# Background work of a two-block transformer kernel is spread over more steps

## The chip, the cores and the metric

The kernel runs on one core of one Trainium2 chip. The metric is the device time of one execution in microseconds (us); lower is better. Times before are the median of three executions, and one further execution was recorded by the hardware profiler.

## The reference, cut to what matters

256 tokens of 1024 features pass through two blocks. The first block has two layers; each is feed-forward, mixer, feed-forward. A feed-forward is `h + 0.5 * (silu(u @ w1) * (u @ w3)) @ w2` with 2816 inner features, on a normalised `u`. So there are four feed-forwards in the first block, here called feed-forward 0 to 3.

The second block has two layers over the tokens and over 256 context tokens. Each starts with a modulation:

```python
mod   = split_cols((sc @ w_mod[l] + b_mod[l])[:, None, :], (D_MODEL,) * N_MOD)
mod_x = split_cols(sc_ctx @ w_mod[l] + b_mod[l], (D_MODEL,) * N_MOD)
```

`sc` and `sc_ctx` are two vectors of 1024 numbers, `w_mod[l]` is 1024 x 6144. The result (table l: shifts, scales and gates) does not depend on the tokens, so it can be computed long before it is used. The same holds for the second block's other tables: the position biases, the sinks and the constants of its layer norms. All arithmetic is fp32.

## The kernel before, in words

**Weights.** All large matrices lie in one stream of 540 tiles of 128x1024, which `Weights` loads by SP's DMA queue into three buffers (`wst`, L270). `prepare` splits each tile into a high part `whi` (ScalarE, ACT, L279) and a low part `wlo` (VectorE, DVE, L280), both kept four deep. `mm3` multiplies a block of 128x128 with three matmuls, high by high, high by low and low by high (L324 to L326).

**A feed-forward of the first block** (`ffn1_layer`) has 22 up steps j, each two weight tiles (48 matmuls), one scaling (L863), a product (L866) and a split of the result (ACT L330, DVE L331), and 8 down steps m with 66 matmuls each and an eviction (L797). After each j and each m it calls `step()`, 30 calls in all; `drain()` at the end calls it until nothing is left.

**Background work.** `step()` advances every generator in `bg` by one `yield`. What a generator issues in a step is placed behind marks: on each engine behind the last split of the layer, on the matmul engine behind the last matmul. Beyond that the compiler's scheduler orders each engine's queue; it may put later independent work first.

- `late_gen` (feed-forward 0) waits four steps, then loads constants and tables. Its three `oneh` tiles share the four buffers `mw` of the modulation. `replicate(0)` then issues eight DMAs of 384 KB on ACT's queue.
- `later_gen` (feed-forward 1) loads the sinks, issues eight such DMAs (`replicate(1)`, read in the odd mixer) and four of 349 KB (`rrep`, read in the second block), and then computes layer-norm constants in small pieces (DVE, and matmuls L458 and L480).
- `mod_gen` computes a table. For table 0 it runs in feed-forwards 0, 1 and 2, with 2048 columns in each, in two groups of 1024 columns (CW). For every 128 rows of a group (k = 0 to 7) it loads a tile `mw` (SP, L708), multiplies by `sc` and adds into the accumulator `macc` on DVE (L724), and does the same for `sc_ctx` with a product on ACT (L727) and an addition on GpSimd (POOL, L728). At k = 0 both products go to ACT (L722). One `yield` follows each k, one follows the group, and then the sum over partitions is taken by matmuls with ones (L736), evicted (L739) and written to DRAM (`modrow`, L741), with one more `yield`: ten steps a group. After the last group the rows are read back (`mt`), transposed (L753) and finished as `modv` and `s1p` (L756 to L761).

**Table 1** is computed in the second block's `ffn2_layer(0)` by `mod_gen(gp, 1, 0, 6 * D, 512, 3)`: twelve groups of 512 columns; the pool gives `macc` one buffer. There a whole group (all eight k) is one step, so that a group has three. That layer calls `step()` 38 times: 6 + 5 + 8 + 11 times in up and down projections and 8 times in `down_gen([0])`. Then come:

```python
            self.drain()
            pre = [self.double_prep(l, 1, 1, 0, i) for i in both]
            self.weave((self.double_gen(l, 1, stats[0], pre[0]), self.DL_STEPS),
                       (self.down_gen([1], gh, gl, evict(True)), KB))
```

`double_prep` reads `modv` and `s1p` of table 1 and makes small weights `dl_w` by transposes (L1320, L1321). `double_gen` turns the statistic of the tokens' rows into `dl_c` (L1340), `rows` and at last the split inputs `HI` and `LO` (L1412, L1413) that the next layer's first weights multiply. `down_gen([1])` is the context's down projection, 264 matmuls that need none of this. Evictions of both down projections are L1543 (`ex` for the tokens, `cx` for the context).

Of the kernel before, what the change touches and what calls it, by code (L numbers as in the profile page):

```python
# [292 lines left out]
class Body:  # L293
# [143 lines left out]
    def later_gen(self):  # L437

        nc, a = self.nc, self.a
        c = self.const  # L440
        self.sink = c.tile([128, 16], FT, name="sink")
        nc.scalar.dma_start(self.sink, _ap(a["row"], ROW_SINK, [[0, 128], [1, 16]]))
        yield
        yield from self.replicate(1)
        self.rrep = self.dram.tile([64, 2 * 6 * 15 * 31], FT, name="rrep")
        for q in range(4):
            nc.scalar.dma_start(self.rrep[16 * q:16 * q + 16], _ap(a["rpb"], 0, [[0, 16], [1, 5580]]))
            yield
        self.nsink = c.tile([128, 16], FT, name="nsink")
        nc.vector.tensor_scalar(self.nsink, self.sink, -1.0, None, op0=OP.mult)  # L450

        ps = self.ps("st")
        o = _VEC["ln1_b"]
        nc.tensor.matmul(ps[:, :32], self.ones, self.vec[:, o:o + 32], start=True, stop=True)
        self.nbb = c.tile([128, 4], FT, name="nbb")
        nc.vector.tensor_reduce(self.nbb, ps[:, :32].rearrange("p (a b) -> p a b", b=8), AX.X, OP.add)
        nc.vector.tensor_scalar(self.nbb, self.nbb, -1.0 / D, None, op0=OP.mult)
        yield  # L458

        self.lnc = c.tile([128, 3, KB, 8], FT, name="lnc")  # L460
        nc.vector.memset(self.lnc, 0.0)
        self.lk = c.tile([128, 3, 4], FT, name="lk")
        for s, (l, which) in enumerate(self.PAIRS):
            g, b = self.ln_cols(l, which)
            w = self.w1()[:, :KB * 4].rearrange("p (m q) -> p m q", q=4)
            nc.vector.tensor_scalar(w[:, :, 0], g, 1.0 / D, None, op0=OP.mult)
            nc.vector.tensor_tensor(w[:, :, 1], w[:, :, 0], g, op=OP.mult)
            nc.vector.tensor_scalar(w[:, :, 3], b, self.nb(l, which), None, op0=OP.add)
            nc.vector.tensor_tensor(w[:, :, 2], w[:, :, 0], w[:, :, 3], op=OP.mult)
            nc.vector.scalar_tensor_tensor(w[:, :, 3], w[:, :, 3], 1.0 / D, w[:, :, 3], op0=OP.mult, op1=OP.mult)  # L470
            lc = self.lnc[:, s]
            for j in (0, 4):
                nc.vector.tensor_scalar(lc[:, :, j], self.ones[:, :KB], 1.0 / D, None, op0=OP.mult)
            nc.vector.tensor_copy(lc[:, :, 1], w[:, :, 0])
            nc.vector.tensor_scalar(lc[:, :, 2], w[:, :, 1], -2.0, None, op0=OP.mult)
            nc.vector.tensor_scalar(lc[:, :, 3], w[:, :, 2], 2.0, None, op0=OP.mult)
            nc.vector.tensor_copy(lc[:, :, 5], w[:, :, 1])
            yield
            ps = self.ps("st")
            nc.tensor.matmul(ps[:, :32], self.ones, w.rearrange("p m q -> p (m q)"), start=True, stop=True)  # L480
            nc.vector.tensor_reduce(self.lk[:, s], ps[:, :32].rearrange("p (m q) -> p q m", q=4), AX.X, OP.add)
            for q, f in ((0, -1.0), (2, -2.0)):
                nc.vector.tensor_scalar(self.lk[:, s, q:q + 1], self.lk[:, s, q:q + 1], f, None, op0=OP.mult)
            yield
        self.rsel = c.tile([32, 3, 128], FR, name="rsel")
        for j, q in enumerate((0, 5, 6)):
            nc.vector.tensor_tensor(self.rsel[:, j], self.ident[:32, q:q + 1].to_broadcast([32, 128]),
                                    self.ident[:32, q + 7:q + 8].to_broadcast([32, 128]), op=OP.add)

        self.lsel = c.tile([128, 8], FT, name="lsel")  # L490
        for k in range(2):
            nc.vector.tensor_tensor(self.lsel[:, 4 * k:4 * k + 4], self.ident[:, 32 * k:32 * k + 4],
                                    self.ident[:, 32 * k + 64:32 * k + 68], op=OP.add)
        self.cc = c.tile([128, 2, 3, 32], FT, name="cc")
        nc.vector.memset(self.cc, 0.0)
        yield
# [196 lines left out]
    def mod_gen(self, pool, l, c0, c1, CW, nb, wait=0):  # L693

        nc = self.nc
        for _ in range(wait):
            yield
        gs = list(range(c0, c1, CW))
        if l:
            gs = gs[4:8] + gs[:4] + gs[8:]  # L700
        todo = [(g, k) for g in gs for k in range(KB)]
        ws = []

        def load():
            if todo:
                g, k = todo.pop(0)
                ws.append(pool.tile([128, CW], FT, name="mw", bufs=nb))
                nc.sync.dma_start(ws[-1], self.a["wmod"][l, k * 128:(k + 1) * 128, g:g + CW])  # L708

        for _ in range(nb - 1):  # L710
            load()
        yield
        for g in gs:
            n = 2 if l == 0 or g < 2 * D else 1
            acc = pool.tile([128, 2, CW], FT, name="macc")
            for k in range(KB):
                load()
                w = ws.pop(0)
                for i in range(n):
                    s = self.sc[:, i * 8 + k:i * 8 + k + 1]  # L720
                    if k == 0:
                        nc.scalar.activation(acc[:, i], w, AF.Copy, scale=s)  # L722
                    elif i == 0:
                        nc.vector.scalar_tensor_tensor(acc[:, i], w, s, acc[:, i], op0=OP.mult, op1=OP.add)  # L724
                    else:
                        t = pool.tile([128, CW], FT, name="mp", bufs=2)
                        nc.scalar.activation(t, w, AF.Copy, scale=s)  # L727
                        nc.gpsimd.tensor_tensor(acc[:, i], acc[:, i], t, op=OP.add)  # L728
                if CW == 1024 or k == KB - 1:
                    yield  # L730
            yield
            w = CW * n // 4
            rows = [(i, c) for i in range(n) for c in range(0, CW, w)]
            ps = self.ps("st")
            for p, (i, c) in enumerate(rows):
                nc.tensor.matmul(ps[32 * p:32 * p + 32, :w], self.ones[:, :32], acc[:, i, c:c + w], start=True,  # L736
                                 stop=True, tile_position=(0, 32 * p), skip_group_check=True)
            mr = self.w2(1)[:, 0, :w]
            nc.scalar.activation(mr, ps[:, :w], AF.Copy)  # L739
            for p, (i, c) in enumerate(rows):  # L740
                nc.sync.dma_start(self.rowd[l][i:i + 1, g + c:g + c + w], mr[32 * p:32 * p + 1])  # L741
            yield
        if c1 == 6 * D:
            mt = pool.tile([128, CW], FT, name="mt", tag="mp", bufs=2)[:96, :128]
            if n == 2:
                nc.sync.dma_start(mt, self.rowd[l].rearrange("i (k c) -> (i k) c", c=128))
            else:
                nc.vector.memset(mt, 0.0)
                nc.sync.dma_start(mt[:48], self.rowd[l][0:1].rearrange("i (k c) -> (i k) c", c=128))
                nc.sync.dma_start(mt[48:64], self.rowd[l][1:2, :2048].rearrange("i (k c) -> (i k) c", c=128))  # L750
            yield
            ps = self.ps("st")
            nc.tensor.transpose(ps[:, :96], mt, self.ident[:96, :96])  # L753
            b = self.vec[:, _VEC["b_mod"] + 48 * l:_VEC["b_mod"] + 48 * l + 48]
            mv = self.modv[l].rearrange("p (i c) -> p i c", i=2)
            nc.vector.tensor_tensor(mv, ps[:, :96].rearrange("p (i c) -> p i c", i=2),  # L756
                                    b[:, None, :].to_broadcast([128, 2, 48]), op=OP.add)
            for half in range(2):
                c = 24 * half + 16
                nc.vector.tensor_scalar(mv[:, :, c:c + 8], mv[:, :, c:c + 8], 1.0 / ALPHA, None, op0=OP.mult)  # L760
                nc.vector.tensor_scalar(self.s1p[l][:, :, half], mv[:, :, 24 * half + 8:24 * half + 16], 1.0, None,  # L761
                                        op0=OP.add)
            yield
# [74 lines left out]
    def ffn1_layer(self, st, nxt, slot, name, idx):  # L838
        nc = self.nc
        with self.tc.tile_pool(name="g" + name, bufs=1) as gp, self.tc.tile_pool(name="mod" + name, bufs=1) as mp:  # L840
# [4 lines left out]
            if idx == 3:  # L845
                self.bg.append(self.ctx_init())
            if idx < 3:
                self.bg.append(self.mod_gen(mp, 0, 2 * D * idx, 2 * D * (idx + 1), 1024, 4, 6 if idx == 0 else 0))
            gh = gp.tile([128, FB, S], FR, name="ghi")
            gl = gp.tile([128, FB, S], FR, name="glo")  # L850
            for j in range(FB):
# [1174 lines left out]
```

## Time and profile before

| | |
|---|---|
| median of 3 executions | 2060.02 us (2059.41 to 2060.64) |
| profiled execution | 2062.72 us, its span 2060.9 us |
| granted clock of the matmul engine, mean | 0.988 |
| HBM read | 351.66 MB, 175 GB/s over the span |

The views used are the page (busy shares of each engine), the windows (busy time, instruction counts, granted clock and DMA share of a stretch), the waits (who released an idle engine), the groups by form (mean duration of one kind of instruction) and the timeline. In a window, "(x694)" after PE is the number of its matmuls.

### The profile page before, as it was taken

The page shows a single profiled execution, that of the slowest core. Times are in us where ns is not written, and L with a number is a line of the kernel's source. Part 1 is how long each engine was busy: PE and PEld are TensorE (multiplying, and loading weights), DVE is VectorE, ACT ScalarE, POOL GpSimd, SP SyncE. Part 2 cuts the span into 40 slices and gives each one's busy share as a digit, 9 for nine tenths or more (in the row PEclk, how much of TensorE's full clock was granted, in tenths as well). Part 3 has the DMA queues.
Part 4 walks back from the last instruction along what each step waited for, and adds up shares of the span by engine and source line. Part 5 has one row for each costly group of instructions (what it writes and reads, how often), then busy time and mean ns, then how long its engine had stood idle before and what let it go on. Part 6 is the DMA issues. An engine that isn't in the chain of part 4 may idle for free. (4 is left out here: it accounts for less than half of the span.)

```text
span 2060.9 us, 39210 instructions
## 1 busy us (share of the span) xinstructions
PE 1989.5 (97%) x15355; PEld 1851.9 (90%) x15355; DVE 1524.9 (74%) x2680; ACT 1134.6 (55%) x2028; POOL 408.4 (20%) x305
## 2 busy tenths in 40 slices
PE   8998999999999999999999999999999999989997
PEld 8988999989999998999999777988888889869997
DVE  6797797998599768886686978666665679776554
ACT  5464587555466548555556866533443455855443
POOL 1223041321033111210330112302230013112002
PEclk9999999999999999999999999999999999999999
DMA  6785645876577563556642323475555653125553
GB/s 219 260 266 171 202 144 184 281 249 215 185 232 229 187 216 110 184 172 188 188 145 73 104 80 118 144 250 169 160 163 164 216 169 103 50 83 156 183 183 103
DMA packets 117114, 355.39 MB, mean 172 GB/s; under 512 B 21782, under 2 KB 27625, under 8 KB 116481
## 3 DMA queue, kind: packets, MB, share of 16 engines
q1 hardware_dynamic: 115472, 344.54, 51.9%
q10 hardware_dynamic: 1456, 8.36, 1.1%
q8 instruction: 120, 1.97, 0.4%
q14 instruction: 66, 0.53, 0.1%
HBM read 351.66 MB, written 8.90 MB: 175 GB/s over the span
## 5 line engine op out<-in xcount | busy, mean ns | idle before, releaser
L280 DVE TENSOR_TENSOR wlo<-wst,whi 128x1024 fp32r<-128x1024 f32 x540 | 709.2, 1314 | 329.4 <-ACT whi L279 327.1
L324 PE MATMUL mm<-HI,whi 128*128 128x256 f32 (+1 forms) x2944 | 865.2, 296 | 12.7 <-ACT whi L279 8.4
L326 PE MATMUL mm<-HI,wlo 128*128 128x256 f32 (+1 forms) x2944 | 863.9, 294 | 6.0 <-DVE wlo L280 6.0
L325 PE MATMUL mm<-LO,whi 128*128 128x256 f32 (+1 forms) x2944 | 865.4, 295 | 1.0 <-DVE LO L1413 0.9
L279 ACT ACTIVATE whi<-wst 128x1024 fp32r<-128x1024 f32 x540 | 570.2, 1056 | 524.8 <-PE mm L325 292.7
L324 PEld LDWEIGHTS mm<-HI,whi 128*128 128x128 f32 x2944 | 564.2, 193 | 38.3 <-issue 11.4
L326 PEld LDWEIGHTS mm<-HI,wlo 128*128 128x128 f32 x2944 | 566.1, 192 | 21.8 <-DVE wlo L280 7.3
L325 PEld LDWEIGHTS mm<-LO,whi 128*128 128x128 f32 x2944 | 566.6, 193 | 18.7 <-issue 6.9
L326 PE MATMUL mm<-ghi,wlo 128*128 128x256 f32 (+1 forms) x1000 | 289.1, 289 | 4.7 <-DVE wlo L280 4.7
L324 PE MATMUL mm<-ghi,whi 128*128 128x256 f32 (+1 forms) x1000 | 287.7, 289 | 1.3 <-ACT ghi L330 1.3
L325 PE MATMUL mm<-glo,whi 128*128 128x256 f32 (+1 forms) x1000 | 288.6, 289 | 0.2 <-DVE glo L331 0.2
L728 POOL TENSOR_TENSOR macc<-macc,mp 128x1024 f32<-128x1024 f32 (+1 forms) x70 | 167.9, 2398 | 447.2 <-ACT mp L727 298.1
L326 PEld LDWEIGHTS mm<-ghi,wlo 128*128 128x128 f32 x1000 | 192.8, 193 | 8.4 <-DVE wlo L280 5.1
L324 PEld LDWEIGHTS mm<-ghi,whi 128*128 128x128 f32 x1000 | 192.4, 193 | 4.3 <-issue 1.5
L325 PEld LDWEIGHTS mm<-glo,whi 128*128 128x128 f32 x1000 | 192.7, 193 | 2.8 <-issue 1.1
L724 DVE SCALAR_TENSOR_TENSOR macc<-mw,sc,macc 128x512 f32<-128x512 f32 (+1 forms) x126 | 168.3, 1336 | 25.6 <-DMA mw<-in_wmod 20.4
L325 PE MATMUL mm<-wlo,HI 128*128 128x256 f32 x352 | 100.6, 286 | 4.0 <-DVE wlo L280 4.0
L324 PE MATMUL mm<-whi,HI 128*128 128x256 f32 x352 | 101.1, 288 | 0.0
L326 PE MATMUL mm<-whi,LO 128*128 128x256 f32 x352 | 100.2, 286 | 0.0
L727 ACT ACTIVATE mp<-mw,sc 128x1024 f32<-128x1024 f32 (+1 forms) x70 | 67.4, 973 | 27.5 <-DMA mw<-in_wmod 18.5
L527 POOL TENSOR_TENSOR sacc<-sacc,w 128x256 f32<-128x256 f32 x36 | 33.6, 932 | 236.7 <-ACT w L523 235.5
L330 ACT ACTIVATE ghi<-w 128x256 fp32r<-128x256 f32 (+1 forms) x120 | 51.1, 426 | 49.8 <-DVE w L866 47.1
(425 smaller groups left out, 2502.5 us busy)
## 6 DMA issues: line engine op xcount, KB each, us to landing
wst<-in_wall SPq DMA_DIRECT2D x540, 512.0 KB
mw<-in_wmod SPq DMA_DIRECT2D x48, 512.0 KB
mw<-in_wmod SPq DMA_DIRECT2D x96, 256.0 KB
brep<-bvec ACTq DMA_DIRECT2D x16, 384.0 KB
nab<-rrep SPq DMA_DIRECT2D x24, 96.0 KB
bias<-brep SPq DMA_DIRECT2D x4, 512.0 KB
bias<-brep SPq DMA_DIRECT2D x8, 256.0 KB
rrep<-in_rpb ACTq DMA_DIRECT2D x4, 348.8 KB
```

The source lines that it names most:

```text
L279: self.marks.append(self.nc.scalar.activation(hi, src, AF.Copy))
L280: self.nc.vector.tensor_tensor(lo, src, hi.bitcast(FT), op=OP.subtract)
L324: nc.tensor.matmul(ps, wh, xh, start=first, stop=False, skip_group_check=True)
L325: nc.tensor.matmul(ps, wh, xl, start=False, stop=False, skip_group_check=True)
L326: self.last = nc.tensor.matmul(ps, wl, xh, start=False, stop=last, skip_group_check=True)
L330: self.marks = [self.nc.scalar.activation(hi, src, AF.Copy), self.nc.vector.tensor_tensor(lo, src, hi.bitcast(FT), op=OP.subtract)]
L527: nc.gpsimd.tensor_tensor(st["acc"], st["acc"], sq, op=OP.add)
L724: nc.vector.scalar_tensor_tensor(acc[:, i], w, s, acc[:, i], op0=OP.mult, op1=OP.add)
L727: nc.scalar.activation(t, w, AF.Copy, scale=s)
L728: nc.gpsimd.tensor_tensor(acc[:, i], acc[:, i], t, op=OP.add)
```

## The change

Two waiting steps instead of six ahead of the modulation in feed-forward 0; a step without work after k = 2 and after k = 5 of a group of 1024 columns; one more step between the end of a group (of any width) and its sum; six steps without work in `later_gen` after its first DMA.

```diff
@@ later_gen
         nc.scalar.dma_start(self.sink, _ap(a["row"], ROW_SINK, [[0, 128], [1, 16]]))
         yield
+        for _ in range(6):
+            yield
         yield from self.replicate(1)
@@ mod_gen
                 if CW == 1024 or k == KB - 1:
                     yield
+                if CW == 1024 and k in (2, 5):
+                    yield
+            yield
             yield
             w = CW * n // 4
@@ ffn1_layer
-                self.bg.append(self.mod_gen(mp, 0, 2 * D * idx, 2 * D * (idx + 1), 1024, 4, 6 if idx == 0 else 0))
+                self.bg.append(self.mod_gen(mp, 0, 2 * D * idx, 2 * D * (idx + 1), 1024, 4, 2 if idx == 0 else 0))
```

## Rows read from the trace of the kernel before

**Rows 1.** The page's first part: busy time, share of the span, instructions.

```profile
PE 1989.5 (97%) x15355; PEld 1851.9 (90%) x15355; DVE 1524.9 (74%) x2680; ACT 1134.6 (55%) x2028; POOL 408.4 (20%) x305
```

**Rows 2.** Windows: us, then PE, PEld, DVE, ACT, POOL busy, PEclk, DMA, GB/s.

```profile
80.00:180.00 100.00, 89.61 (x694) 86.33 (x693) 94.44 (x85) 56.66 (x75) 40.84 (x14) 0.95 0.70 236
400.00:500.00 100.00, 90.79 (x720) 87.03 (x719) 89.94 (x137) 53.30 (x72) 25.40 (x10) 0.97 0.71 239
580.00:680.00 100.00, 99.33 (x820) 97.32 (x819) 95.74 (x96) 60.66 (x81) 41.66 (x14) 1.00 0.72 227
1880.00:1980.00 100.00, 100.00 (x836) 100.00 (x835) 54.56 (x70) 46.48 (x70) 0.00 (x0) 1.00 0.57 184
```

**Rows 3.** Waits of PE in 80 to 180 and 400 to 500: total us, times, longest.

```profile
PE mm L326 <- DVE wlo L280: 9.0, 5, 3.5
...
PE st L480 <- DVE w L470: 5.0, 3, 2.3
```

**Rows 4.** Groups by form on DVE, last layer; L863 from 80 to 180.

```profile
L280 DVE TENSOR_TENSOR wlo<-wst,whi 128x1024 fp32r<-128x1024 f32 x35 | 42.9, 1225 | 46.2 <-ACT whi L279 46.2
L1509 DVE TENSOR_TENSOR w<-w,mm 128x256 f32<-128x256 f32 x18 | 7.5, 414 | 0.0
L331 DVE TENSOR_TENSOR glo<-w,ghi 128x256 fp32r<-128x256 f32 x17 | 7.1, 419 | 0.0
...
L863 DVE TENSOR_TENSOR w<-mm,rstd 128x512 f32<-128x512 f32 x12 | 8.2, 679 | 0.1
```

**Rows 5.** Timeline of DVE in feed-forward 0: start, duration, instruction.

```profile
94.58 1.27 DVE L724 SCALAR_TENSOR_TENSOR macc<-mw,sc,macc 128x1024 f32<-128x1024 f32 x1
...
99.32 3.43 DVE L724 SCALAR_TENSOR_TENSOR macc<-mw,sc,macc 128x1024 f32<-128x1024 f32 x1
```

**Rows 6.** Timeline of POOL in feed-forwards 1 and 2.

```profile
371.03 2.44 POOL L728 TENSOR_TENSOR macc<-macc,mp 128x1024 f32<-128x1024 f32 x1 [18.96 <-ACT mp L727]
...
413.11 2.35 POOL L728 TENSOR_TENSOR macc<-macc,mp 128x1024 f32<-128x1024 f32 x1 [3.60 <-ACT mp L727]
...
592.43 3.31 POOL L728 TENSOR_TENSOR macc<-macc,mp 128x1024 f32<-128x1024 f32 x1 [3.05 <-ACT mp L727]
598.80 3.31 POOL L728 TENSOR_TENSOR macc<-macc,mp 128x1024 f32<-128x1024 f32 x1 [3.05 <-ACT mp L727]
```

**Rows 7.** Window of feed-forward 0 ahead of the modulation's first group.

```profile
40.00:60.00 20.00, 20.00 (x163) 19.23 (x162) 12.53 (x17) 8.47 (x12) 0.00 (x0) 1.00 0.58 180
```

**Rows 8.** Timeline of PE at the end of down_gen([1]).

```profile
1671.85 0.28 PE L326 MATMUL mm<-ghi,wlo 128*128 128x256 f32 x1
...
1676.46 0.79 PE L1394 MATMUL tp<-rows,dl_w 32*128 32x256 f32 x2 [3.78 <-DVE h L1410]
```

**Rows 9.** Timeline of DVE in ffn2_layer(0), up projection and end.

```profile
1565.01 0.75 DVE L724 SCALAR_TENSOR_TENSOR macc<-mw,sc,macc 128x512 f32<-128x512 f32 x1 [1.08 <-DMA mw<-in_wmod]
...
1631.96 0.48 DVE L1543 SCALAR_TENSOR_TENSOR ex<-mm,modv,ex 128x256 f32<-128x256 f32 x1 [0.30 <-PE mm L326]
...
1653.32 0.26 DVE L756 TENSOR_TENSOR modv<-st,vec 128x96 f32<-128x96 f32 x1 [0.50 <-PE st L753]
...
1661.78 0.16 DVE L1340 COPY dl_c<-tp 128x16 f32<-128x16 f32 x1
...
1677.34 0.90 DVE L1413 TENSOR_TENSOR LO<-h,HI 128x256 fp32r<-128x256 f32 x1
```

**Rows 10.** Timeline of PE: the sums of table 1's last three groups.

```profile
1602.31 0.43 PE L736 MATMUL st<-macc,ones 128*32 128x128 f32 x8
...
1624.29 0.42 PE L736 MATMUL st<-macc,ones 128*32 128x128 f32 x8
...
1644.06 0.43 PE L736 MATMUL st<-macc,ones 128*32 128x128 f32 x8
```

**Rows 11.** Timeline of ACT: a group's first product, and the small weights.

```profile
1553.64 0.70 ACT L722 ACTIVATE macc<-mw,sc 128x512 f32<-128x512 f32 x1
...
1660.29 1.08 ACT L1321 ACTIVATE dl_w<-tp 96x512 fp32r<-96x512 f32 x2
```

## The prediction

> **What bounds the kernel now.** The page's busy shares come first: TensorE (PE) is busy 97% of the span, VectorE (DVE) 74% [rows 1]. So time can only come from stretches in which PE is short of work, and the next view is the windows. In the last layer, where nothing runs beside the weights, PE issues 836 matmuls in 100 us, 0.1196 us each, with no idle time [rows 2]; a step of the up projection (48 matmuls) is 5.74 us. In the three layers that carry the first modulation (table 0), the same 100 us hold 694, 720 and 820 matmuls [rows 2], while DVE is busy 94, 90 and 96 us instead of 55. PE stands idle there for 10.4, 9.2 and 0.7 us, and the granted clock falls to 0.95 and 0.97 after these stops: parts of the windows ran at 1.2 GHz instead of 2.4. The waits name the releasers: the split weights wlo in the first layer, the later tables' small DVE work in the second [rows 3]. DVE is thus what limits PE in these stretches, and only there.
>
> Why DVE is late: without modulation a step needs two splits of 1.225 us, 0.68 for the up pair's scaling, 0.41 and 0.42 for product and split [rows 4], 3.96 us of the 5.74. A modulation step adds one DVE multiply-add, 1.27 us alone, but 3.43 when it meets the GpSimd (POOL) add of the step before [rows 5]. What a full step then takes is read from POOL's adds: six intervals from 371.03 to 413.11 us, 7.01 us each, in the second layer; 6.37 us in the third [rows 6].
>
> **The change, part by part.**
>
> *Rests in a group of 1024 columns (all three layers).* Before, steps k=1 to 7 follow each other: at 7.01 us DVE falls behind by 1.27 a step, 8.9 us in seven, and only then come two light steps. At 6.37 us it is 0.63 a step, 4.4 us in seven, and that layer loses only 16 matmul slots (1.9 us) [rows 2, 6]: some 4 to 5 us of backlog is carried by the split tiles that lie ready. After, a light step gives back 5.74 - 3.96 = 1.78: k=1,2 reach 2.5, the rest leaves 0.8, k=3 to 5 reach 4.6, the rest leaves 2.8, k=6,7 reach 5.3, and three light steps (one is the sum's new wait) give back 5.3. The peak is what the third layer carries now, so nearly all stops should go. Their worth: idle 20.3 us plus the clock, 5% and 3% of 100 us, together 28.3 us; by slots 142 + 116 + 16 = 274, times 0.1196, 32.8 us, which includes the sums' own matmuls that stay. I take a gain of **28 us** (ends: 10, from rival D, and 33). What is late next in these layers is PE itself.
>
> *First layer: two waiting steps instead of six.* The group's 16 weight loads and their work begin four steps sooner, beside the constants' loads. DVE is busy 12.5 of 20 us there and the DMA engines 0.58 [rows 7], so both have room. late_gen's three oneh tiles come out of the same four buffers as the modulation's weights, now while these are in use; a load may then wait a step, and two rests take that up. Nothing, -1 to +2 us. The start is needed, since the two groups now take 26 steps; 2 + 1 + 26 = 29 fit in the layer's 30. The modulation's loads share SP's queue with the weights; a load whose buffer DVE or ACT still reads holds the weight load behind it, and with DVE less late these stops get shorter. POOL's queue holds the same adds, spread wider; the next norm's small adds stand behind them only in the down projection.
>
> *Second layer: later_gen six steps later.* Twelve DMAs on the ACT queue (brep, rrep) and the small DVE and PE pieces move from steps 2 to 21 to 8 to 27. The readers come layers later, so nothing waits. The pieces behind PE's 5.0 us of waits [rows 3] then stand half in the down projection, whose steps are 66 matmuls (7.9 us). That is in the 28.
>
> *Second block: the sum's extra wait is not tied to 1024 columns.* This is the price. mod_gen for table 1 has 512 columns, twelve groups of three steps: 1 + 36 + 1 = 38, exactly the 38 steps of ffn2_layer(0), with the last transpose drained. Now a group has four: the ninth sum (group 8) falls on step 37, group 9's multiply-adds on step 38, and drain() issues that sum, both remaining groups and the transpose. Behind it stand double_prep, which reads modv, and double_gen, whose LO the next block's first slabs need; the only other PE work is down_gen([1]). The cover is small: its last matmul starts at 1671.85, and PE then waits 3.78 us for DVE already [rows 8].
>
> Worked out: step 37 ends with the seventh of down_gen([0])'s m-steps, whose eviction is at 1631.96 [rows 9]; group 8's sum comes there. Three rounds follow in series, because one accumulator (macc) must be summed before the next group's first product. Rounds now, sum to sum, take 21.98 and 19.77 us [rows 10]. The multiply-adds alone, in a calmer stretch, run from 1553.64 to 1565.76, 12.1 us [rows 9, 11]; the rest of a round is the sum, which waits its turn in PE's order. I take 17 for the two rounds beside down_gen([1]), between 12.5 and 20.9, and 12 for the last, when PE and the DMA engines are free: 46. Sum to modv is 9.3 us now (1644.06 to 1653.32) [rows 9, 10]: two short DMAs, one after the other, and a transpose that stands among matmuls; with PE free I take 6.7. From modv to the first LO is 24.0 us now (1653.32 to 1677.34), dl_w at 1660.29 and dl_c at 1661.78 on the way [rows 9, 11]. Weight splits, evictions and down_gen([1])'s matmuls stand between in every queue, and LO does not come before the last of those. With them gone I take 15 (ends 12 and 24). LO: 1632 + 46 + 6.7 + 15 = 1699.7, against 1677.3: a loss of **22 us** (ends: 1632 + 37.5 + 6.7 + 12 gives 11; 1632 + 62.7 + 9.3 + 24 gives 51). Nothing of the next block can fill it. The clock after so long a stop: nothing, 0 to 3, since PE stops there now as well.
>
> *Sum.* The profiled execution took 2062.7 us (span 2060.9), 2.7 above the median of the runs, 2060.0. 2062.7 - 28 + 22 = 2056.7; on the median's scale **2054**.
>
> **The rivals.** A measurement of this kernel can tell about 0.2%, 4.1 us, so "same" is 2055.9 to 2064.1.
>
> *B, the drain costs more (slower).* Place: the three rounds at the end of ffn2_layer(0). If they keep today's 20.9 us, R is 62.7, the loss 39, and the time 2060 - 28 + 39 = 2071. It decides from a mean round of 17.2 us on (with my other terms the loss is three rounds less 23.6, and 28 is then reached). For it: both rounds in that stretch are longer [rows 10], and down_gen([1]) loads as many weights as down_gen([0]). Against: the multiply-adds themselves need 12.1 us, and the last round runs alone.
>
> *C, the drain is half hidden (faster still).* If double_gen's statistics, which read nothing of modv, are put ahead of the late modulation and the rounds run at 12.5, then modv to LO is about 10 us and the loss 37.5 + 6.7 + 10 - 45.3 = 9: 2041. For it: the instruction order is the scheduler's, not the program's alone. Against: dl_c follows dl_w now [rows 9, 11], though it needs only a finished statistic, as if PSUM tiles of one tag were handed out in the program's order.
>
> *D, the rests are too few (slower).* If every POOL add costs DVE its own 2.4 us whole [rows 6], a full step is 3.96 + 1.27 + 2.40 = 7.63, the backlog grows by 1.89 a step and reaches 9.7 us in the new pattern; 4.4 above the 5.3 that I take as carried, in four groups, is 18 us. Gain 10, time 2060 - 10 + 22 = 2072. This is what the Trainium skill's page "SBUF — State Buffer" (section "Who interferes with whom") would make of it: a DVE instruction with two SBUF inputs and a GpSimd one that reads SBUF exclude each other for a whole instruction. The trace agrees for single instructions (1.27 against 3.43), but the step of 6.37 us says that much of it falls into time that DVE or POOL wait anyway.
>
> **How the numbers follow.** My case 0.50 (own range, by gains of 25 to 31 and losses of 17 to 29, 2046 to 2064; faster 0.34, same 0.13, slower 0.03); B 0.22 (slower 0.20, same 0.02); C 0.12, faster; D 0.16 (slower 0.12, same 0.04). Faster 0.46, same 0.19, slower 0.35. The range takes in the middles of B, C and D: 2039 to 2075.
>
> **What would show it.** Right: about 820 matmuls or more in the 100 us windows of the first two layers, clock 1.00, waits for wlo and L480 gone; against it a PE gap of some 25 us near the end of ffn2_layer(0), modv about 53 us after the eviction at which group 8's sum stands (now 21), ended by h or LO. Wrong: windows that stay near 720 (D), rounds of over 18 us (B), or modv early enough that PE waits under 10 us (C).

## The result and the profile after

The changed kernel takes 2079.77 us (median of 6 runs, 2074.46 to 2084.58), the kernel before 2059.72 us (6 runs, 2055.18 to 2062.79): a ratio of 1.0094, 95% interval 1.0079 to 1.0108. The change made the kernel 20 us slower; 2054.0 was forecast, and the range ended at 2075. The profiled execution of the changed kernel took 2075.63 us (span 2073.8, mean granted clock 0.983), 4.1 below its median, that of before 3.0 above its own; so the two traces differ by 12.9 us only. Sizes below are from medians unless a trace is named.

In the changed kernel later lines have moved: L724 is L726, L727 L729, L728 L730, L736 L741, L753 L758, L480 L482, L756 L761, L1413 L1418, L1543 L1548.

The page's first part, of the kernel after (of before: [rows 1]):

```profile
PE 1985.6 (96%) x15355; PEld 1850.5 (89%) x15355; DVE 1524.6 (74%) x2680; ACT 1136.4 (55%) x2028; POOL 406.3 (20%) x305
```

Busy time hardly moved, so the 12.9 us are PE standing idle or slowed. The windows of the three modulation layers come next (columns as in [rows 2]), and one of the end of `ffn2_layer(0)`; kernel after:

```profile
80.00:180.00 100.00, 93.54 (x755) 91.17 (x754) 88.81 (x86) 56.39 (x76) 32.53 (x12) 0.98 0.73 240
400.00:500.00 100.00, 94.71 (x765) 93.33 (x764) 88.42 (x126) 54.47 (x74) 24.99 (x10) 0.97 0.72 241
580.00:680.00 100.00, 100.00 (x834) 99.03 (x833) 91.77 (x96) 60.48 (x82) 29.62 (x10) 1.00 0.72 227
...
1655.00:1700.00 45.00, 18.21 (x125) 12.54 (x124) 26.25 (x87) 12.02 (x29) 7.98 (x7) 0.62 0.35 103
```

The same end in the kernel before:

```profile
1655.00:1700.00 45.00, 41.22 (x332) 37.02 (x331) 36.16 (x114) 24.54 (x53) 9.88 (x9) 0.92 0.53 164
```

The matmuls in the three windows rose from 694, 720 and 820 [rows 2] to 755, 765 and 834: the third layer is full, the first two are repaired in part. What is left there, by the waits of PE (20 to 240 us, then 340 to 560; total us, times, longest), kernel after, against 9.0 and 5.0 [rows 3]:

```profile
PE mm L326 <- DVE wlo L280: 6.6, 5, 3.3
...
PE st L482 <- DVE w L472: 4.0, 1, 4.0
```

At the end of `ffn2_layer(0)` PE issues 125 matmuls in 45 us where it issued 332, at a mean granted clock of 0.62: that is where the gain and more was lost.

To place gains and losses to a few tenths, I counted the large matmuls (L324 to L326), which every kernel here issues in the same number and layer by layer in the same order, and took the start of the n-th in each trace, less its start in the trace of before. The profiled times of all kernels, in us:

```
                    n =   1584   3960   5544  10560  11088    end
                        end of: FFN0   FFN1   FFN2  (ahead of, behind the stop)
before, start           224.9  555.9  752.7 1596.9 1682.5
after                    -6.6  -11.3  -12.9  -16.5  +11.7  +12.8
e1 wide only             -6.1   -9.5  -11.0  -11.8  -11.6  -11.8
e2 narrow alone          -1.6   +1.9   +1.9   -0.5  +26.9  +29.0
e3 tables back           -5.4   -8.3   -9.9  -11.7  -11.0  -11.2
e4 no POOL additions    -16.6  -29.5  -32.9  -35.1  -34.7  -34.9
e5 both on DVE          -15.3  -28.9  -32.3  -34.1  -34.4  -34.6
e6 three rests           -2.8   +0.3   +4.8   +5.6   +4.9   +4.7
e7 e5, fewer steps      -15.9  -29.4  -32.9  -31.1  -36.5  -34.1
e8 before, both on DVE  -16.2  -28.0  -29.1  -31.4  -30.9  -31.2
e9 after, both on DVE   -15.7  -28.7  -32.1  -35.9   -3.5   -2.9
e10 no rests             -8.9  -16.1  -17.8  -19.1  -18.9  -19.2
e11 sum's wait alone     -0.9   -0.1   -1.8   -3.0   -3.6   -3.8
e12 e10, both on DVE    -15.8  -28.2  -30.4  -31.4  -31.4  -31.6
```

Read the line of after: 12.9 us gained over the three layers, 16.5 by 1597 us, and 28.2 lost between matmul 10560 and 11088. Some 2 to 3 of the 3.6 us between the third layer and 1597 us belong to the narrow groups' wait itself: e2, which has nothing else, gains 2.4 there, after 3.6, e1 without that wait 0.8.

### The profile page after: what moved, and what is told of

Read it like the earlier page. It is cut to its first block, busy times and chain, and to the rows that moved or that the text cites. A ratio compares the mean times of both kernels' runs of the same rounds, so it can differ in the third digit from the quotient of the medians.

```text
span 2073.8 us, 39200 instructions
## 1 busy us (share of the span) xinstructions
PE 1985.6 (96%) x15355; PEld 1850.5 (89%) x15355; DVE 1524.6 (74%) x2680; ACT 1136.4 (55%) x2028; POOL 406.3 (20%) x305
## 5 line engine op out<-in xcount | busy, mean ns | idle before, releaser
L324 PE MATMUL mm<-HI,whi 128*128 128x256 f32 (+1 forms) x2944 | 862.5, 295 | 13.3 <-ACT whi L279 8.4
L326 PE MATMUL mm<-HI,wlo 128*128 128x256 f32 (+1 forms) x2944 | 861.5, 294 | 3.6 <-DVE wlo L280 3.6
L324 PEld LDWEIGHTS mm<-HI,whi 128*128 128x128 f32 x2944 | 562.0, 192 | 36.5 <-issue 11.9
L326 PEld LDWEIGHTS mm<-HI,wlo 128*128 128x128 f32 x2944 | 564.0, 192 | 19.2 <-DVE wlo L280 4.7
L326 PE MATMUL mm<-ghi,wlo 128*128 128x256 f32 (+1 forms) x1000 | 289.9, 290 | 6.0 <-DVE wlo L280 6.0
L324 PE MATMUL mm<-ghi,whi 128*128 128x256 f32 (+1 forms) x1000 | 288.6, 289 | 0.2 <-ACT ghi L330 0.2
L730 POOL TENSOR_TENSOR macc<-macc,mp 128x1024 f32<-128x1024 f32 (+1 forms) x70 | 165.8, 2369 | 550.7 <-ACT mp L729 357.4
L326 PEld LDWEIGHTS mm<-ghi,wlo 128*128 128x128 f32 x1000 | 193.1, 193 | 10.8 <-DVE wlo L280 6.8
L324 PEld LDWEIGHTS mm<-ghi,whi 128*128 128x128 f32 x1000 | 192.8, 193 | 5.1 <-issue 3.4
L726 DVE SCALAR_TENSOR_TENSOR macc<-mw,sc,macc 128x512 f32<-128x512 f32 (+1 forms) x126 | 172.4, 1368 | 17.8 <-DMA mw<-in_wmod 14.3
L324 PE MATMUL mm<-whi,HI 128*128 128x256 f32 x352 | 101.8, 290 | 0.0
L326 PE MATMUL mm<-whi,LO 128*128 128x256 f32 x352 | 101.2, 288 | 0.0
L729 ACT ACTIVATE mp<-mw,sc 128x1024 f32<-128x1024 f32 (+1 forms) x70 | 67.2, 972 | 14.9 <-POOL macc L730 7.5
L870 ACT ACTIVATE w<-w 128x256 f32<-128x256 f32 x88 | 36.2, 412 | 69.4 <-DVE w L868 67.9
```

The lines of the kernel that those rows point to most:

```text
L324: nc.tensor.matmul(ps, wh, xh, start=first, stop=False, skip_group_check=True)
L326: self.last = nc.tensor.matmul(ps, wl, xh, start=False, stop=last, skip_group_check=True)
L870: nc.scalar.activation(sl, t[:, 0], AF.Silu)
```

## The experiments

**e1: the drain taken away.** The extra step ahead of the sum is tied to 1024 columns, so that table 1 again needs 38 steps.

```diff
@@ mod_gen, kernel after
-            yield
+            if CW == 1024:
+                yield
             yield
```

> The change with the sum's extra wait for groups of 1024 columns alone, so that table 1 ends within its 38 steps as before. Theory (the drain is the whole loss): nth matmul for nth matmul the changed kernel was 16.5 us ahead of the one before up to the last down projection of the second block's first layer and lost 28 to 29 us there, so this one keeps the 16 us: about 2043 to 2046, PE's gap there back to about 4 us, windows of the first block as in the changed kernel (755, 765, 834 matmuls). Rival (the longer median of the changed kernel, 20 us where its profile shows 13, comes from the first block's new order or from the clock there): this one stays at 2055 or above.

Measured 2049.54 us (2048.21 to 2051.28), ratio to before 0.9963 (0.9949 to 0.9978). The drain cost 2079.8 - 2049.5 = 30.2 us, and the rest of the change gained 10 (8 by the ratio), where 28 was forecast. That is short of the theory's 2043 to 2046, since a part of the 16.5 us came from the narrow groups' wait, which e1 does not have.

**e2: the drain alone.** The kernel before with the step for narrow groups only.

```diff
@@ mod_gen, kernel before
+            if CW == 512:
+                yield
             yield
```

> The kernel before with one thing of the change: groups of 512 columns wait one step more ahead of their sum. Theory: the first block is as before, and the drain costs three rounds of about 17, 16 and 12 us after group 8's sum: 28 to 29 us in the profile, up to 36 with a longer stretch at half clock: 2088 to 2096. Rival (the loss needs the rests or the moved tables, through the order of the whole queue): under 2075.

Measured 2088.88 us (2083.61 to 2095.87), ratio 1.0156 (1.0132 to 1.0181): 29.3 us more than before, without any other part of the change.

**e3: the tables where they were.** e1 without the six steps in `later_gen`.

```diff
@@ later_gen, e1
-        for _ in range(6):
-            yield
```

> As the first, but the second block's tables begin at once in their layer as before. Theory: the stop of PE at 466 to 500 us in the changed kernel (5.3 us idle, 3.4 us of clock) comes from the moved table pieces, which now meet k = 5 to 7 of the second group; back at steps 16 to 20 they meet its first steps with little backlog, and the kernel is 3 to 8 us faster than the first, about 2038 to 2042. Rival (DMA): the tables' twelve DMAs beside the first group cost weights, whi waits for its loads, and the kernel is 2 us or more slower than the first.

Measured 2051.21 us (2047.16 to 2053.88), ratio 0.9962 (0.9949 to 0.9975), the same as e1. In the table the second layer alone gives 2.9 us (8.3 - 5.4) against 3.4 in e1. Beside rests, where the small work stands makes no difference that these runs can tell, so neither theory nor rival came.

**e4: no additions on POOL.** e1 without the line that adds the context's product; the context's sum is left out, its products are still made on ACT.

```diff
@@ mod_gen, e1
                         nc.scalar.activation(t, w, AF.Copy, scale=s)
-                        nc.gpsimd.tensor_tensor(acc[:, i], acc[:, i], t, op=OP.add)
```

> As the first, without POOL's additions into the context's accumulator (the context's modulation is then the last product of k = 0 alone). Theory (the rests are too few because a POOL add stops DVE): DVE's multiply-add is back at 1.27 us and the splits at 1.23, and the stops of PE that are left in feed-forward 0 and 1 (6.5 and 5.3 us idle in their 100 us) go: 820 or more matmuls in each 100 us, 10 to 15 us faster than the first in the profile. Rival (the scheduler bunches the adds, or later_gen's pieces stop PE whatever POOL does): the stops stay within 2 us.

Measured 2028.31 us in one run. The windows of e4 and one group of DVE, 80 to 180 us (busy us and mean ns behind the bar):

```profile
80.00:180.00 100.00, 100.00 (x834) 99.03 (x833) 75.17 (x93) 62.31 (x84) 2.84 (x3) 1.00 0.77 257
400.00:500.00 100.00, 100.00 (x834) 99.03 (x834) 73.83 (x137) 58.88 (x77) 2.64 (x3) 1.00 0.74 244
580.00:680.00 100.00, 100.00 (x834) 99.03 (x834) 72.98 (x92) 59.66 (x80) 1.25 (x2) 1.00 0.68 221
```

```profile
L726 DVE SCALAR_TENSOR_TENSOR macc<-mw,sc,macc 128x1024 f32<-128x1024 f32 x11 | 14.1, 1279 | 0.0
```

PE stops nowhere, and every multiply-add takes its 1.28 us. DVE is busy for 75 us of 100 instead of 88, though it does the same work: the rest was time in which a POOL addition held up a DVE instruction, rival D's mechanism, called the lock from here on. All that was left of the stops in these layers came from POOL's additions.

**e5: both multiply-adds on DVE.** If the addition costs DVE more than it takes off it, DVE should do the work itself. Same result as before.

```diff
@@ mod_gen, e1
-                    elif i == 0:
-                        nc.vector.scalar_tensor_tensor(acc[:, i], w, s, acc[:, i], op0=OP.mult, op1=OP.add)
                     else:
-                        t = pool.tile([128, CW], FT, name="mp", bufs=2)
-                        nc.scalar.activation(t, w, AF.Copy, scale=s)
-                        nc.gpsimd.tensor_tensor(acc[:, i], acc[:, i], t, op=OP.add)
+                        nc.vector.scalar_tensor_tensor(acc[:, i], w, s, acc[:, i], op0=OP.mult, op1=OP.add)
```

> As e1 (the sum's extra wait for 1024 columns alone), but the context's accumulation is a second multiply-add on DVE in place of ACT's product and POOL's addition; the result is the same. DVE gets more work of its own: 2 x 1.28 us a step, 6.5 us in a full step against PE's 5.74. Theory (the port lock in bursts, not DVE's amount of work, is what the rests cannot cover): no instruction of DVE takes 3.4 us any more, the stops of PE go as in e4, and the time is 2028 to 2035. Rival (DVE's amount of work decides): a full step of 6.5 us is no shorter than the 6.4 to 7.0 us with POOL, stops stay as in e1, 2045 to 2052.

Measured 2029.76 us (2028.53 to 2031.17), ratio 0.9855 (0.9840 to 0.9869), faster than both kernels. Its windows:

```profile
80.00:180.00 100.00, 100.00 (x824) 98.06 (x823) 87.80 (x105) 50.28 (x74) 4.59 (x3) 1.00 0.77 261
400.00:500.00 100.00, 100.00 (x835) 99.03 (x834) 84.32 (x146) 49.63 (x69) 4.10 (x3) 1.00 0.73 248
580.00:680.00 100.00, 100.00 (x834) 99.03 (x833) 85.28 (x103) 49.92 (x72) 0.80 (x1) 1.00 0.69 221
```

DVE does twice the multiply-adds and is busy no longer than in the kernel after (88.81, 88.42, 91.77), with PE at 100.00. So DVE's share alone does not stop PE. ACT's relief is not the reason either: e4 kept ACT's products and was as fast.

The rival was put with a wrong price, though. The 6.5 us are a sum of durations, and in the timelines each DVE instruction starts some 0.07 us before the end given for the one ahead of it. By the starts, with DVE never idle between, a full step with two multiply-adds takes 5.93 us, in e5's second layer:

```profile
381.72 2.48 DVE L726 SCALAR_TENSOR_TENSOR macc<-mw,sc,macc 128x1024 f32<-128x1024 f32 x2
...
387.65 2.48 DVE L726 SCALAR_TENSOR_TENSOR macc<-mw,sc,macc 128x1024 f32<-128x1024 f32 x2
```

With one multiply-add that meets no addition it takes 4.74 (94.58 to 99.32 in [rows 5]). So e5 has shorter full steps than the 6.4 to 7.0 with POOL as well as no long instructions, and it does not tell which of the two counts; that the additions are the cause, e4 and e5 show together.

**e6: three rests.** Rests after k = 1, 3 and 5, no extra wait of the sum: the same 13 steps in another cut.

```diff
@@ mod_gen, e1
-                if CW == 1024 and k in (2, 5):
+                if CW == 1024 and k in (1, 3, 5):
                     yield
-            if CW == 1024:
-                yield
             yield
```

> As e1, with POOL as there, but three rests in a group, after k = 1, 3 and 5, and no extra wait ahead of the sum: the same 13 steps, never more than two full steps in a row. Theory of the prediction (a backlog that grows step by step and is given back by rests): its peak falls from 5.3 to about 2.5 us, and most of the stops left in e1 go: 2040 or below. Rival (single bursts of POOL adds and multiply-adds, 6.8 to 10 us long where the instruction order puts two together, stop PE whatever the mean pace): within 3 us of e1, 2047 to 2052.

Measured 2066.65 us (2065.74 to 2067.64), ratio 1.0036 (1.0022 to 1.0049): neither theory nor rival, 17 us slower than e1. Some 3 of these can belong to the sum's extra step, which e6 lacks (e11); the rest is the other cut. POOL's timeline in e6 shows what neither had:

```profile
159.03 13.28 POOL L730 TENSOR_TENSOR macc<-macc,mp 128x1024 f32<-128x1024 f32 x4 [3.06 <-ACT mp L729]
...
491.55 8.23 POOL L730 TENSOR_TENSOR macc<-macc,mp 128x1024 f32<-128x1024 f32 x3 [6.26 <-ACT mp L729]
...
695.02 9.03 POOL L730 TENSOR_TENSOR macc<-macc,mp 128x1024 f32<-128x1024 f32 x3 [6.00 <-ACT mp L729]
```

By the count of matmuls the down projections begin at 150.3, 478.5 and 686.3 us here: in each layer the last full steps now fall into them, and there three or four additions stand one behind the other. The code has a reason for it (argued from it, not tried): a step is held behind the layer's last split, and in the down projection nothing is split, so that every step called there is free at once. A third rest pushed more work into that place. In the first layer four full steps are called there, against three in e1.

**e7: table 1 a step sooner.** e5 with two steps instead of three for each narrow group; the question was whether PE's last short stop, 1641 us, can be had too.

```diff
@@ mod_gen, e5
             if CW == 1024:
                 yield
-            yield
+                yield
```

> As e5, and table 1's groups of 512 columns take two steps instead of three, so that modv of table 1 is ready before the last down projections. Theory: double_gen's chain then runs beside down_gen([1]); PE's gap of about 4 us there and the stretch of 6.8 us at half clock go, 5 to 9 us faster than e5. Rival (LO waits for the end of down_gen([1])'s statistic or for its queue anyway): within 2 us of e5.

Measured 2030.08 us (2028.89 to 2030.97), ratio 0.9857 (0.9840 to 0.9874): as e5, within the rival's 2 us, but not for its reason. In the trace the stop is gone: PE has no idle time there and the full clock, and the table gains 5.4 us between matmul 10560 and 11088 (0.3 in e5); LO comes at 1632.0, ahead of the context's last eviction (1644.1). But against e5 it loses 3.6 us between the third layer and that place and 2.6 after it; what takes these was not tried.

**e8: DVE alone, none of the change.** The kernel before with e5's edit of the multiply-adds.

> The kernel before with that second multiply-add on DVE and nothing of the change: no rests, the old starts. Theory of the lock: seven steps of 6.5 us put DVE behind by 5.3 us, about what the lead carries, so most of e5's gain comes without any rest: 2033 to 2042. Rival (rests are what is needed once the lock is gone): 2048 or above, and e5 clearly faster than this.

Measured 2033.68 us (2031.85 to 2034.53), ratio 0.9872 (0.9857 to 0.9887). The edit brings 25 us by itself (by 5.93 us a step, seven full steps put DVE 1.3 us behind PE, not 5.3); the rests, the start, the sum's wait and `later_gen`'s steps together add about 4 to it, and the intervals of e5 and e8 overlap.

**e9: the drain without POOL.** e5 with the narrow groups' extra step put back, that is, the whole change with e5's edit.

> The whole change, drain included, with the second multiply-add on DVE instead of ACT's product and POOL's addition (the same result). The drain of table 1 is thus put back into the kernel that measured 2029.8 us. Theory: the stop at the end of ffn2_layer(0) does not depend on table 0 or on POOL; it costs its 30 us again: 2058 to 2061 us. Rival: a part of the 30 us, some 8, comes because table 1's rounds are late behind their steps on account of POOL's additions there; with those gone the eighth sum comes some 6 us sooner and the rounds are shorter, the loss is near the 22 us of the prediction: 2050 to 2053 us.

Measured 2059.91 us (2057.71 to 2063.00), ratio 0.9998 (0.9987 to 1.0009), 30.15 us more than e5. The stop does not depend on POOL; in the program the last four groups have no context part, and so no additions. PE's timeline of e9, the sums of the last four groups:

```profile
1608.94 0.43 PE L737 MATMUL st<-macc,ones 128*32 128x128 f32 x8
...
1626.87 0.43 PE L737 MATMUL st<-macc,ones 128*32 128x128 f32 x8
...
1640.38 0.66 PE L737 MATMUL st<-macc,ones 128*32 128x128 f32 x8 [4.84 <-DVE macc L726]
...
1652.60 0.65 PE L737 MATMUL st<-macc,ones 128*32 128x128 f32 x8 [11.57 <-DVE macc L726]
```

**e10: no rests.** e1 without the two rests; the sum's wait for 1024 columns, the sooner start and `later_gen`'s six steps stay.

```diff
@@ mod_gen, e1
-                if CW == 1024 and k in (2, 5):
-                    yield
```

> The change without the two rests after k = 2 and k = 5 and without the narrow groups' wait; what stays is the sum's extra step in a group of 1024 columns, the start four steps sooner and later_gen's six steps. Theory: what gains 10 us is that the rests keep full steps from following each other, so that the bursts on DVE find PE with a lead; without them the gain is gone: 2057 to 2061 us. Rival: the rests give nothing, the sum's extra step (no matmul queue waits for DVE's last addition) and the earlier start give the 10 us: 2048 to 2052 us.

Measured 2041.79 us (2039.54 to 2043.66), ratio 0.9913 (0.9897 to 0.9928): 8 us faster than with the rests (10 by the ratios), and beyond the rival too. POOL in e10, the second group of the first layer:

```profile
120.55 2.40 POOL L730 TENSOR_TENSOR macc<-macc,mp 128x1024 f32<-128x1024 f32 x1 [25.98 <-ACT mp L729]
127.75 3.35 POOL L730 TENSOR_TENSOR macc<-macc,mp 128x1024 f32<-128x1024 f32 x1 [4.79 <-ACT mp L729]
134.15 3.30 POOL L730 TENSOR_TENSOR macc<-macc,mp 128x1024 f32<-128x1024 f32 x1 [3.06 <-ACT mp L729]
...
159.58 3.30 POOL L730 TENSOR_TENSOR macc<-macc,mp 128x1024 f32<-128x1024 f32 x1 [3.05 <-ACT mp L729]
```

Seven additions, one a step, 6.4 us apart from the second on, the last one ahead of the first eviction of the down projection (163.9), and none in a row. PE stops behind this group for 1.4 us (158.4 and 159.5), for ACT's and DVE's split of the product. In the first group two additions stand in a row, at 88.69, and the longest stop of PE in this layer, 3.29 us, comes right after them (96.84). The second group in the kernel before, first fence, ends in a run of four, and in e11, second fence, in one of five:

```profile
160.66 13.28 POOL L728 TENSOR_TENSOR macc<-macc,mp 128x1024 f32<-128x1024 f32 x4 [3.05 <-ACT mp L727]
```

```profile
160.45 16.61 POOL L728 TENSOR_TENSOR macc<-macc,mp 128x1024 f32<-128x1024 f32 x5 [3.06 <-ACT mp L727]
```

**e11: the sum's wait alone.** The kernel before with an extra step ahead of the sum in groups of 1024 columns.

```diff
@@ mod_gen, kernel before
+            if CW == 1024:
+                yield
             yield
```

> The kernel before with one thing alone: in groups of 1024 columns the sum waits one step more. No rests, the start after six steps and later_gen as before. The kernel with this, the start after two steps and later_gen's six steps, but no rests, measured 2041.8, 19 less than before; by its trace 8.9 of that came in the first layer, 7.2 in the second, 1.7 in the third. Theory: the first layer's share belongs to the start (with it the second group's last full steps lie in the up projection, not in the first steps of the down projection, where additions are put together and stop PE), the rest to the sum's wait: 2049 to 2053 us. Rival: the sum's wait alone gives all of it: 2040 to 2044 us. Second rival: the start and later_gen's steps give all of it and the sum's wait nothing: 2057 to 2062 us.

Measured 2056.36 us (2054.07 to 2059.11), ratio 0.9985 (0.9974 to 0.9995): 3 us, nearer to the second rival than to the theory. It takes away PE's wait for the accumulator (in the table 1.7 us in the third layer, -0.1 to -1.8; all three layers together 1.8), and it pushes the second group of the first layer further into the down projection, five additions in a row. Between e11 and e10 stand only the start and `later_gen`: some 15 us together. By the table 8.0 of it lie in the first layer (-0.9 and -8.9), where `later_gen` does not run yet: that is the start. Another 8.0 lie in the second (+0.8 and -7.2), where the start is over; whether `later_gen`'s steps alone bring these was not tried.

**e12: both on DVE, no rests.** e10 with e5's edit.

> The kernel with both multiply-adds of the modulation on DVE (2029.8 us, the same result) without the two rests. Theory: the rests cost 8 us only because they push full steps into the down projection, where POOL's additions come in bursts; without POOL there are no such bursts, PE is busy all the time either way, and the time stays: 2029 to 2031 us. Rival: the rests are harmful by themselves, or their two steps were needed: 2020 to 2024, or 2033 to 2036 us.

Measured 2031.58 us (2031.06 to 2032.21), ratio 0.9858 (0.9842 to 0.9874): as e5. Without POOL the rests do not hurt; a help of up to 2 us (the difference of the medians, with overlapping intervals) is not excluded.

## Why the prediction was wrong

Two terms carried it: a gain of 28 us in the first block and a loss of 22 at the end of `ffn2_layer(0)`. Measured: 10 (e1) and 30 (after less e1; e2 29.3, e9 30.2). The sign turned on the first; of the 26 us that the forecast was short, 18 are in it and 8 in the second.

**What failed: "Rests in a group of 1024 columns".** The step took a mean pace for each full step, let the light steps give time back, and so came to a peak of 5.3 us that the split tiles carry. The rests measured as a loss of 8 us (e1 less e10; 10 by the ratios). Three things were wrong in it. (Its light step of 3.96 us, a sum of durations, is too long as well, 3.5 by the starts; but that would give back more, not less.)

First, the long stops of PE come not from a slow sum but from a short run of blocked instructions, which a mean pace does not show. DVE in the kernel after, in the first layer, and further down in the second:

```profile
154.80 1.23 DVE L280 TENSOR_TENSOR wlo<-wst,whi 128x1024 fp32r<-128x1024 f32 x1 [1.39 <-ACT whi L279]
155.95 0.42 DVE L331 TENSOR_TENSOR glo<-w,ghi 128x256 fp32r<-128x256 f32 x1
156.28 6.82 DVE L726 SCALAR_TENSOR_TENSOR macc<-mw,sc,macc 128x1024 f32<-128x1024 f32 x2
163.03 3.35 DVE L280 TENSOR_TENSOR wlo<-wst,whi 128x1024 fp32r<-128x1024 f32 x1
...
475.17 0.11 DVE L468 TENSOR_SCALAR w<-vec 128x8 f32<-128x8 f32 x1
475.18 2.45 DVE L470 TENSOR_SCALAR w<-vec,nbb 128x8 f32<-128x8 f32 x1
477.54 1.27 DVE L726 SCALAR_TENSOR_TENSOR macc<-mw,sc,macc 128x1024 f32<-128x1024 f32 x1
```

POOL over the same stretches:

```profile
147.86 2.40 POOL L730 TENSOR_TENSOR macc<-macc,mp 128x1024 f32<-128x1024 f32 x1 [7.12 <-ACT mp L729]
156.27 9.03 POOL L730 TENSOR_TENSOR macc<-macc,mp 128x1024 f32<-128x1024 f32 x3 [6.00 <-ACT mp L729]
...
475.21 2.39 POOL L730 TENSOR_TENSOR macc<-macc,mp 128x1024 f32<-128x1024 f32 x1 [4.86 <-ACT mp L729]
```

And PE behind them:

```profile
166.43 0.58 PE L326 MATMUL mm<-ghi,wlo 128*128 128x256 f32 x1 [3.28 <-DVE wlo L280]
...
481.21 0.64 PE L482 MATMUL st<-w,ones 128*128 128x32 f32 x2 [3.96 <-DVE w L472]
```

Three additions in a row take 9.03 us; in that time DVE finishes two multiply-adds (6.82 instead of 2 x 1.27) and a split (3.35 instead of 1.22), and PE runs dry. Just before, at 154.80, DVE had waited 1.39 us for ACT, and ACT 1.31 us for PE (153.71): DVE had been ahead as far as it could be. Time that light steps give back cannot be stored beyond the four tiles of `whi` and `wlo`. The run accounts for 3.28 of the 7.0 us that PE is idle in this layer. Another 2.4, in the first group, follow on additions that come singly (98.90 and 104.58), after ACT had waited 4.5 us for a weight tile. The stop in the second layer is the lock only in part: in e10 L470 met no addition (0.22 us), and PE still waited 1.96 us for that chain.

Second, the rests lengthen the group, and with them the second group's last steps fall into the down projection's first, where additions come in a row: three at 156.27 in the kernel after, four in e6, none in e10. In the kernel before it was four, on account of the late start. That the place in the down projection is what joins the additions is argued from these counts and the program, not shown by a run of its own; e12 shows that without additions the rests cost nothing.

Third, a group without rests falls into an even beat of 6.4 us (e10 above, and [rows 6] for the third layer), in which the addition meets a split; the first step after a pause takes 7.2 (120.55 to 127.75), and rests make more of these. What the full steps lose at 6.4 us was carried but for little, as the prediction said of the third layer: in e10 the second groups of the first and third layers end with stops of 1.4 and 1.2 us, the third layer's first group with none. Rests do no harm by themselves either: the third layer of the kernel after has them and is full (834).

**"First layer: two waiting steps instead of six ... Nothing, -1 to +2."** This was the second error: by the table the start brings some 8 us, because the second group's steps then all lie in the up projection (e10 against e11, without rests). The prediction saw that it "is needed" to fit the steps, and did not look at which projection they fall in. **The sum's wait** brings 3 (e11; 1.8 of it in the three layers); in the prediction it was one of three light steps.

**Rival D** had the gain right, 10, and the lock as the reason; it expected a total of 2072 because it kept the loss of 22. By the lock as the Trainium skill has it on the page "SBUF — State Buffer" (section "Who interferes with whom"), whichever of the two engines issues first holds the other for its whole instruction. The trace agrees: 1.27 becomes 3.4 [rows 5], a split of 1.22 becomes 3.35. The same page of the Trainium skill counts tensor_scalar among the operations that can block. L470 agrees: 128x8 numbers, 2.45 us beside an addition of 2.39, and 0.22 later, at 506.38, beside none. D's step of 7.63 has the same fault as the 3.96: by the starts it is 4.74 + 2.2 = 6.9 where an addition meets the multiply-add, which is the second layer's 7.0, and 6.36 where it meets a split. What D did not see is that nearly the whole 28 was to be had by taking the addition off POOL (e8, 25).

**The loss: right in kind, its start mis-sized.** The prediction's sum, against the trace of after moved by the 16.5 us that this kernel is ahead there. PE first, then DVE, kernel after:

```profile
1622.15 0.42 PE L741 MATMUL st<-macc,ones 128*32 128x128 f32 x8
...
1639.45 0.43 PE L741 MATMUL st<-macc,ones 128*32 128x128 f32 x8
...
1655.73 0.42 PE L741 MATMUL st<-macc,ones 128*32 128x128 f32 x8
...
1667.66 0.65 PE L741 MATMUL st<-macc,ones 128*32 128x128 f32 x8 [11.50 <-DVE macc L726]
1672.39 0.39 PE L758 MATMUL st<-ident,mt 96*128 96x96 f32 x1 [4.08 <-issue]
...
1684.84 0.63 PE L1387 MATMUL tp<-ident,cc 128*96 128x128 f32 x2 [6.79 <-DVE cc L1351]
```

```profile
1617.07 0.48 DVE L1548 SCALAR_TENSOR_TENSOR ex<-mm,modv,ex 128x256 f32<-128x256 f32 x1 [0.30 <-PE mm L326]
1617.47 0.74 DVE L726 SCALAR_TENSOR_TENSOR macc<-mw,sc,macc 128x512 f32<-128x512 f32 x1
1620.95 0.48 DVE L1548 SCALAR_TENSOR_TENSOR ex<-mm,modv,ex 128x256 f32<-128x256 f32 x1 [0.58 <-PE mm L326]
...
1672.82 0.26 DVE L761 TENSOR_TENSOR modv<-st,vec 128x96 f32<-128x96 f32 x1 [1.52 <-PE st L758]
...
1689.46 1.83 DVE L1418 TENSOR_TENSOR LO<-h,HI 128x256 fp32r<-128x256 f32 x2
```

Rounds 17.3, 16.3 and 11.9 us (predicted 17, 17, 12); sum to `modv` 5.2 (6.7); `modv` to LO 16.6 (15). Together these are 0.4 us less than predicted. The start is not: group 8's sum was put at the seventh eviction, 1632 on the clock of before; it came at 1622.15 + 16.5 = 1638.7. That eviction is at 1617.07, but the group's last multiply-add runs at 1617.47, behind it, and the sum stands in PE's order behind the last matmuls of the eighth step. Of the 6.7 us, 1.6 are the eviction itself, 1.1 the last product (to 1618.2) and 4.0 PE's order. In e9 it is 1608.94 + 35.9 = 1644.8. A sum waits for its products and for its place among PE's matmuls, not only for its step. With 6.7 more and 0.4 less the 22.4 become 28.7, what the trace shows (28.2); medians give 29 to 30. Rival B had the longer rounds as its reason, which did not come; neither did rival C's, rounds of 12.5 and 10 us from `modv` to LO.

**The "clock after so long a stop: 0 to 3".** By the trace's record of the granted clock it stood at 1.2 GHz for 34.1 us from 1661.1 on, but PE stands idle for most of that, and runs at the low level only from LO (1689.5) to 1695.2. The kernel before has the same: 1.2 GHz from 1676.2 to 1683.0, 5.7 us from its LO (1677.3) on. So the term came out as it was taken, nothing.

**The marks.** "About 820 matmuls or more in the first two layers, waits gone" failed (755 and 765, 6.6 us of wlo and 4.0 of L482 left); "a PE gap of some 25 us, `modv` about 53 us after that eviction" came as said, `modv` 55.75 us (1617.07 to 1672.82), PE idle for 26.8 us in six pieces between 1656.2 and 1688.2.

## What to carry to other kernels

Before work that makes an engine late is spread in time, look in the trace for what lengthens its single instructions, and for runs of them: here taking the additions off POOL was worth 25 us in the kernel before (e8), 20 in e1 and in the kernel after (e5, e9) and 10 in e10 (e12), spreading them in rests less than nothing. An addition given to POOL cost DVE more, 1.6 us where it met a split (2.83 against 1.21) and 2.2 where it met a multiply-add (3.43 against 1.27), than the 1.28 of doing that work on DVE. And where a generator shares one step count with another stage, as tables 0 and 1 do here, count the steps for every caller: one extra `yield` cost 30 us in the stage that was full.

## What the runs showed that was not expected

A DVE instruction on 128x8 numbers takes 2.4 us where it meets a POOL addition, eleven times its usual 0.22, so small work that looks free is not. Twice the multiply-adds on DVE (e5) left its busy share where it was, 84 to 88 of 100 us, because it no longer waits inside its instructions: a busy share counts the lock as work. And an even beat of full steps, 6.4 us against PE's 5.74, passed the first group of e10's third layer without a stop, so a step longer than PE's need not be cut up.
